# Turning h for the gate product by DMA blocks and VectorE 32x32 transposes in a gated decoder layer

## The chip, the cores and the metric

The kernel runs on one core of a Trainium2 chip. The metric is device time in microseconds of one execution; lower is better. Five engines work side by side and meet through semaphores: TensorE (PE; its weight loads are PEld), VectorE (DVE), ScalarE (ACT), GpSimd (POOL) and SyncE (SP), which here only issues DMAs. Each engine runs its own instructions in the order of the program, so one that waits holds up all that stand behind it on that engine.

## What is computed

One layer of a decoder trunk for 1024 prompt tokens and 8 sample tokens, with D = 1024, in float32. Cut to what matters here:

```python
m = sigmoid(g_a) * (y_a @ w_pa) + sigmoid(g_b) * (y_b @ w_pb)
h = h + rmsnorm(m @ w_out, post_g)
e = p @ w_ple
gate = sigmoid(rmsnorm(h, ple_in_g) @ w_pg)
h = h + rmsnorm(gate * e, ple_out_g)
```

where `rmsnorm(x, g) = x * rsqrt(mean(x * x) + 1e-6) * g` over the 1024 features. The products that make y_a, y_b, g_a and g_b come before and are not touched, save for their order on some engines.

## The kernel before

**Products.** Each float32 operand is cut into a high and a low part (`split`, L412: ACT copies, DVE subtracts), and three of the four partial products are run. Most 2x2 block products are done with seven block products instead of eight (`strassen`, L691; `strassen_within`, L740). The last two, the out product (m by w_out) and the gate product (h by w_pg), put tokens on the output partitions: the weights that PE loads are 128 x 128 blocks of m or h turned so that features lie on partitions, and w_out or w_pg stream past. Both go over four pairs of token tiles (tile t is tokens 128t to 128t+127), each pair with seven steps named by the operand they use: B11, T2, T3, T1, B21, B22, T4 (the last pair ends with B22). A step is twelve matmuls of 512 columns. `outsteps[0..3]` are followed by `gatesteps[0..3]`; `oflow` and `gflow` are these 28 and 28 steps as flat lists. The loaded weights are prepared three steps ahead (`AHEAD`): `mw` from m, `hw` from h, with `ms` and `hs` for the sums and differences. In each pair the T2 result must first have the B11 result added by DVE and be copied out by ACT before the T1 step may accumulate on it in the same PSUM region (L754 to L759).

**From the out product to the gate product.** For every token tile t the results are gathered in `h` with a sum of squares by ACT. `out_finish` (L1505) takes the root (DVE adds, POOL raises to -1/2: `rstd`, L453), scales by DVE and lets a POOL DMA add the input x in place (`accum_op`); SP then writes h to DRAM, where the last residual sum takes it from. `gate_norm` (L1514) takes the sum of squares of this h over 1024 columns by ACT, the root again, and writes `hn`, the normalised h, by ACT. `gate_input` (L1522) turns hn by eight PE transposes of 128 x 128 into two PSUM banks (`pht`), and ACT copies each bank to `big`, the buffer with features on partitions from which hw is cut. Feature k*128+p lies on partition p of row k of `big`. The rows of w_pg were multiplied by ple_in_g by ACT early on (`column_sums`, L1455, `wgraw`) and stored in DRAM as `wg`, `wglow` and `wghigh`. `gated` (L1548) applies the sigmoid to the product by ACT, multiplies by e (`eback`) by DVE, and takes the sum of squares. The 8 sample tokens (tile S) go through small matmuls of their own (`sps`), hung on steps from `oflow[OS]` and `gflow[GS]` on.

**What sets the order.** All code from the first matmul on is recorded in a `Planner` (L86). Each recorded operation has a time `at` (the PE work recorded until then), a latest time, and buffers. The planner then plays through its own durations and picks for each engine the ready operation with the least rank, `min(late, at + PATIENCE)` (L285), and may start loads `LOAD` ahead of their latest time (L274). Work hung on a step with `at(step, f)` (L1340) is recorded after that step. The order that comes out is fixed in the program; nothing is decided on the chip. 46 buffers of 128 x 1032 floats (`slot`) are handed out by the planner. Nearly every instruction has the line of the player, L354.

## Time and profile before

| what | value |
|---|---|
| time, median of three runs | 989.72 us (988.19 to 990.26) |
| the profiled execution's own time | 989.02 us |
| its span, first to last instruction | 987.3 us |
| mean granted TensorE clock | 0.998 |
| DVE, ACT, POOL busy | 793.4, 514.5, 72.6 us |
| DMA | 181.62 MB, mean 184 GB/s |

All times in what follows are those of this one profiled execution, in us from the start of its span unless a number is said to be a duration. A tile's instructions are grouped by engine and operation, with least, median and greatest duration in ns. In the chain of waits each piece is the work, or the wait, without which the last instruction would have come sooner. In the table by windows, the busy time of each engine stands beside the number of its instructions.

### The profile page before, as it was taken

What the parts mean: (1) busy time and instruction counts of PE and PEld (TensorE: products, weight loads), DVE (VectorE), ACT (ScalarE), POOL (GpSimd) and SP (SyncE); (2) the same over time, 40 slices, a digit from 0 to 9 for tenths busy, and PEclk for the clock granted to TensorE, in tenths of its full rate; (3) what the DMA queues carried; (4) which work ended last, traced back from release to release, by engine and by line L of the source; (5) the groups of instructions that cost most, each with busy time, mean ns of one, the idle gap of its engine ahead of it and who ended that gap; (6) DMA issues with size and microseconds to landing.
All of it is one profiled execution on the core that took longest, in us unless ns stands there. A gap on an engine that the chain in (4) does not pass through costs nothing.

```text
span 987.3 us, 15941 instructions
## 1 busy us (share of the span) xinstructions
PE 975.2 (99%) x6113; PEld 865.0 (88%) x6113; DVE 793.4 (80%) x1229; ACT 514.5 (52%) x861; POOL 72.6 (7%) x117
## 2 busy tenths in 40 slices
PE   8999999999999999999999999999999999999996
PEld 6889999999999999999999999999999986787765
DVE  5698469878889789887686997697799899678866
ACT  7774356766435544242332433562363364899744
POOL 1210000000000000000010100000000002222221
PEclk9999999999999999999999999999999999999999
DMA  9364654433475777441214176684582485489496
GB/s 355 135 150 87 150 127 153 150 97 122 168 275 195 277 282 253 150 162 54 87 54 153 33 240 233 242 318 158 183 302 86 167 325 133 104 268 327 104 307 193
DMA packets 123489, 181.62 MB, mean 184 GB/s; under 512 B 41222, under 2 KB 80182, under 8 KB 123405
## 3 DMA queue, kind: packets, MB, share of 16 engines
q1 hardware_dynamic: 121077, 172.71, 51.4%
q0 software_dynamic: 2048, 7.37, 4.1%
q8 instruction: 48, 0.79, 0.3%
q10 hardware_dynamic: 288, 0.52, 0.2%
q14 instruction: 28, 0.23, 0.1%
HBM read 125.08 MB, written 55.96 MB: 183 GB/s over the span
## 4 chain that ended last, share of the span: by engine, by line
PE 97%; DVE 1%; POOL 0%; ACT 0%; issue 0%; DVEq 0%; POOLq 0%
PE acc L354 73%; PE acct L354 15%; PE accm L354 2%; PE e L354 2%; PE mix L354 1%; PE sps L354 1%; PE pht L354 1%; PE pst L354 1%; POOL rstd L354 0%; DVE ge L354 0%; PE warm L354 0%; DVE hs L354 0%; DVE hw L354 0%; PE pp L354 0%; DVE wgT4l L354 0%
## 5 line engine op out<-in xcount | busy, mean ns | idle before, releaser
L354 DVE TENSOR_TENSOR u<-acc,u 128x520 f32<-128x520 f32 (+1 forms) x90 | 62.5, 695 | 33.3 <-PE acc L354 32.5
L354 POOL TENSOR_TENSOR rstd<-ms,mhalf 128x1 f32<-128x1 f32 (+1 forms) x45 | 39.6, 882 | 493.6 <-DVE ms L354 493.5
L354 ACT ACTIVATE u<-acc 128x512 f32<-128x512 f32 x39 | 23.2, 596 | 36.2 <-PE acc L354 33.7
L354 ACT ACTIVATE zbw<-zbs 128x512 fp32r<-128x512 f32 x16 | 10.0, 630 | 31.4 <-DVE zbs L354 25.6
L354 DVE TENSOR_TENSOR big<-big 128x1024 f32<-128x1024 f32 (+4 forms) x20 | 23.6, 1215 | 0.0
L354 POOL COPY big<-xb 128x1 f32<-128x1 f32 x8 | 4.0, 494 | 259.8 <-DVE zbw L354 149.4
L354 ACT ACTIVATE pbw<-pbs 128x512 fp32r<-128x512 f32 x16 | 10.1, 632 | 24.3 <-DVE pbs L354 19.0
L354 ACT ACTIVATE paw<-pas 128x512 fp32r<-128x512 f32 x16 | 10.1, 629 | 23.3 <-DVE pas L354 16.2
L354 DVE TENSOR_TENSOR zbw<-zbs,zbw 128x512 fp32r<-128x512 f32 x16 | 10.9, 688 | 13.7 <-ACT zbw L354 13.6
L354 PE MATMUL accm<-qh,wpoolw 128*128 128x260 f32 (+1 forms) x96 | 20.9, 319 | 0.0
L354 ACT ACTIVATE big<-mix 128x256 f32<-128x256 f32 x32 | 11.9, 382 | 17.0 <-PE mix L354 16.2
L354 ACT ACTIVATE gbw<-gbs 128x512 fp32r<-128x512 f32 x16 | 10.1, 630 | 16.6 <-DVE gbs L354 10.6
L354 ACT ACTIVATE u<-acct 128x512 f32<-128x512 f32 x22 | 13.0, 593 | 8.8 <-PE acct L354 5.4
L354 DVE SCALAR_TENSOR_TENSOR zb<-accm,gvec,zb 128x512 f32<-128x512 f32 (+1 forms) x16 | 12.0, 750 | 6.7 <-PE accm L354 6.4
L354 PEld LDWEIGHTS accm<-qh,wpoolw 128*128 128x128 f32 x96 | 15.6, 188 | 1.9
L354 ACT ACT_TABLE_LOAD x11 | 14.1, 1283 | 4.7 <-DMA wohigh<-woraw 1.9
L354 DVE TENSOR_TENSOR ge<-eback,ge 128x512 f32<-128x512 f32 (+2 forms) x19 | 12.4, 658 | 5.1 <-ACT ge L354 4.5
L354 ACT ACTIVATE gaw<-gas 128x512 fp32r<-128x512 f32 x16 | 10.0, 628 | 12.2 <-PE acc L354 7.5
L354 DVE TENSOR_TENSOR paw<-pas,paw 128x512 fp32r<-128x512 f32 x16 | 11.0, 687 | 6.1 <-ACT paw L354 6.1
L354 PE MATMUL mix<-wst,vh 128*128 128x256 f32 x64 | 15.5, 319 | 0.0
L354 ACT ACTIVATE gbw<-gbraw 128x512 fp32r<-128x512 f32 x12 | 7.5, 628 | 15.0 <-DMA gbraw<-in_w_in_dram 10.3
L354 ACT ACTIVATE zaw<-zas 128x512 fp32r<-128x512 f32 x16 | 10.1, 628 | 9.3 <-DVE zas L354 5.1
(664 smaller groups left out, 3575.0 us busy)
## 6 DMA issues: line engine op xcount, KB each, us to landing
ga<-ga SPq DMA_DIRECT2D x16, 516.0 KB, 7.2
gb<-gb SPq DMA_DIRECT2D x16, 516.0 KB, 7.6
ya<-za SPq DMA_DIRECT2D x8, 516.0 KB, 4.7
yb<-zb SPq DMA_DIRECT2D x8, 516.0 KB, 7.3
x<-in_x_prompt_dram SPq DMA_DIRECT2D x8, 512.0 KB, 5.6
vraw<-in_w_in_dram SPq DMA_DIRECT2D x8, 512.0 KB, 8.2
e<-e SPq DMA_DIRECT2D x8, 512.0 KB, 2.9
vturned<-v SPq DMA_DIRECT2D x32, 128.0 KB, 3.2
```

The source lines that it names most:

```text
L354: getattr(getattr(self.nc, e), method)(*(self.real(a) for a in args), **{k: self.real(a) for k, a in kwargs.items()})
```

## The change

h is no longer normalised before it is turned, and PE no longer turns it.

- `gate_input` reads h back from DRAM, where `out_finish` has put it. Four DMAs of SP per token tile, each to 32 partitions, bring 256 features each: partition 32q+f gets, for each of four groups i of 32 tokens, the 256 features from 256q on of token 32i+f. One DVE instruction then turns all 32 x 32 blocks of the tile, into `big`. So feature 256q+32k+f now lies on partition 32q+f of row k.
- The rows of w_pg are loaded in this same order, by four DMAs of 32 rows instead of one of 128 (`wgraw`), ple_in_g likewise, and for the sample tokens ACT writes hn in the new order.
- `gate_norm` takes the sum of squares in two halves of 512 columns and puts the root into a column of `hscales`; the write of hn falls away for the prompt tokens. The sigmoid takes that column as its scale, one number per token, which is a partition there.
- The steps on which the three parts are hung come from the table `TURNS`, one row per pair, as indices into `oflow + gflow`; before they were 7, 8, 13; 14, 15, 20; 21, 22, 27; 28, 29, 34. While these parts are recorded the planner's patience is 8 (`HASTE`).
- The planner's LOAD goes from 14.0 to 14.98 and PATIENCE from 60.0 to 55.8, for the whole kernel. The sample work starts two steps later in the out product and two earlier in the gate product (OS, GS), and the loads of w_pg's sums one step earlier.

```diff
+HASTE = 8.0
+TURNS = ((7, 8, 11), (14, 14, 18), (21, 26, 28), (30, 33, 35))
-OS, GS = 3, 14
+OS, GS = 5, 12
...
-    LOAD, LEAD, PATIENCE, RATE, SPARE = 14.0, 14.0, 60.0, 0.36, 3
+    LOAD, LEAD, PATIENCE, RATE, SPARE = 14.98, 14.0, 55.8, 0.36, 3
...
             op = Op(engine, len(self.ops), self.clock, self.fixed)
+            op.patience = self.patience
...
-            return min(o.late, o.at + self.PATIENCE) + (3.0 if o.table and o.table != table else 0)
+            return min(o.late, o.at + o.patience) + (3.0 if o.table and o.table != table else 0)
...
-            dma(t, src[k * P : (k + 1) * P, :])
-            if key == "wg":
+            if key == "wo":
+                dma(t, src[k * P : (k + 1) * P, :])
+            else:
+                for q in range(4):
+                    dma(t[32 * q : 32 * q + 32, :], src[(8 * q + k) * 32 : (8 * q + k + 1) * 32, :])
                 nc.scalar.activation(out=t, in_=t, func=AF.Copy, scale=col(2, k))
...
-        hn = hn_of[t] = slot("hn", (P, D))
-        rs = rstd([square_sum(h[:r], r, scratch=hn)], r)
-        nc.scalar.activation(out=hn[:r], in_=h[:r], func=AF.Copy, scale=rs[:r])
+        if t == S:
...
+            return
+        parts[t] = []
+        for j in range(2):
+            gather(parts[t], square_sum(h[:, half(j)]))
+        scales[t] = rstd(parts.pop(t), P, hscales[:, t : t + 1])
...
-        for k4 in range(0, NB, 4):
-            ps = bank("pht")
-            for k in range(4):
-                nc.tensor.transpose(ps[:, k * P : (k + 1) * P], hn[:, (k4 + k) * P : (k4 + k + 1) * P], ident)
-            nc.scalar.activation(out=big[:, k4 : k4 + 4, t * P : (t + 1) * P],
-                                 in_=ps.rearrange("p (k t) -> p k t", k=4), func=AF.Copy)
+        b, src = slot("hblocks", (P, D)), kept["h"][t * P : (t + 1) * P, :]
+        for q in range(4):
+            dma(b[32 * q : 32 * q + 32, :].rearrange("f (i c) -> f i c", i=4),
+                src[:, 2 * q * P : (2 * q + 2) * P].rearrange("(i f) c -> f i c", i=4))
+        nc.vector.transpose(out=big[:, :, t * P : (t + 1) * P].rearrange("p k (i f) -> p k i f", i=4),
+                            in_=b.rearrange("p (i k f) -> p k i f", i=4, k=NB))
...
-        nc.scalar.activation(out=g, in_=src, func=AF.Sigmoid)
+        nc.scalar.activation(out=g, in_=src, func=AF.Sigmoid, scale=1.0 if t == S else scales[t])
...
-    turn_over(wgop, [*outsteps[2][5:], *l], [*l[2:], c[0], c[1]], WITHIN)
+    turn_over(wgop, [*outsteps[2][4:], *l], [*l[2:], c[0], c[1]], WITHIN)
...
-        nxt = outsteps[i + 1] if i + 1 < NPAIR else gatesteps[0]
         ts = [2 * i + 1, 2 * i]
-        at(nxt[0], lambda ts=ts: [out_finish(t) for t in ts])
-        at(nxt[1], lambda ts=ts: [gate_norm(t) for t in ts])
-        at(nxt[6], lambda ts=ts: [gate_input(t) for t in ts])
+        for do, s in zip((out_finish, gate_norm, gate_input), TURNS[i]):
+            at((oflow + gflow)[s], lambda do=do, ts=ts: hasty(do, ts))
```

Over the whole program PE loses 64 transposes and gains nothing. DVE gains 8 transposes of 128 x 1024 and 8 instructions on one column. ACT loses 16 copies of a PSUM bank, 8 writes of hn and 8 sums of squares over 1024 columns, and gains 16 sums over 512. POOL's count stays. SP gains 32 reads of h and 24 loads of w_pg rows. The numbers behind an underscore in the rows below tell apart tiles of one name.

PE at the start of the gate product, from the B11 step of pair 0 to its T2 step, before:

```order
L354 MATMUL acct_574<-wgB11l_9299,hw_9292 128x512
L354 MATMUL acct_574<-wgB11h_9280,hw_9292 128x512
L354 MATMUL pht_570<-ident,hn_9376 128x128 x4
L354 MATMUL pht_571<-ident,hn_9376 128x128 x4
L354 MATMUL acct_579<-wgT2h_9297,hw_9344 128x512
L354 MATMUL acct_579<-wgT2l_9328,hw_9344 128x512
```

The same place of PE now:

```order
L357 MATMUL acct_569<-wgB11l_9320,hw_9285 128x512
L357 MATMUL acct_569<-wgB11h_9273,hw_9285 128x512
L357 MATMUL acct_570<-wgT2h_9294,hw_9371 128x512
L357 MATMUL acct_570<-wgT2l_9355,hw_9371 128x512
L357 MATMUL acct_570<-wgT2h_9294,hw_9371 128x512 x2
```

The eight transposes of a tile of pair 2 stood between the two steps; now the steps follow each other. The other seven groups of eight go in the same way.

DVE in the same stage, before: `acct` is the sum on the T2 result that T1 waits for, `ge_9573` the sum that frees the region of the T4 step, `h_9395` and `h_9352` the scaled h of pair 3.

```order
L354 SCALAR_TENSOR_TENSOR h_9395<-h_9395,rstd_578,post_8587 128x1024
L354 TENSOR_TENSOR hw_9426<-hs_9364,hw_9426 128x512
L354 SCALAR_TENSOR_TENSOR h_9352<-h_9352,rstd_576,post_8587 128x1024
L354 TENSOR_TENSOR wgT1l_9459<-wgT_1270_9272,wgT1h_9450 128x1024
L354 TENSOR_TENSOR wgT1l_9471<-wgT_1271_9277,wgT1h_9456 128x1024
L354 TENSOR_TENSOR acct_579<-acct_579,u_9466 128x512
L354 TENSOR_TENSOR hw_9475<-hs_9316,hw_9475 128x512
L354 TENSOR_TENSOR wgB21l_9496<-wgB_1286_9301,wgB21h_9482 128x1024
L354 TENSOR_TENSOR wgB21l_9505<-wgB_1287_9305,wgB21h_9490 128x1024
```

DVE at this place now:

```order
L357 TENSOR_TENSOR wgT1l_9418<-wgT_1260_9241,wgT1h_9341 128x1024
L357 TENSOR_TENSOR wgT1l_9429<-wgT_1261_9251,wgT1h_9377 128x1024
L357 TENSOR_TENSOR hw_9350<-hs_9337,hw_9350 128x512
L357 TENSOR_TENSOR wgB21l_9442<-wgB_1268_9277,wgB21h_9400 128x1024
L357 TENSOR_TENSOR wgB21l_9453<-wgB_1269_9283,wgB21h_9410 128x1024
L357 TENSOR_SCALAR sofar_561<-ssq_559 128x1
L357 TENSOR_SCALAR ms_562<-ssq_560,sofar_561 128x1
L357 TENSOR_TENSOR acct_570<-acct_570,u_9435 128x512
```

Pair 3's two scalings have gone from here (they stand some twenty rows further on, ahead of the first transpose of pair 2), and two cuts of B21 stand ahead of the sum on T2.

SP from the first h written to the loads of w_pg's operands, before:

```order
L354 DMA h<-h_8801 128x1024
L354 DMA h<-h_8762 128x1024
L354 DMA h<-hs_8972 8x1024
L354 DMA h<-h_8937 128x1024
L354 DMA h<-h_8990 128x1024
L354 DMA wgB_1248_9174<-wg 128x2x512
L354 DMA wgB_1249_9178<-wg 128x2x512
L354 DMA wgT_1253_9196<-wglow 128x2x512
```

SP at this place now, where `hblocks` are the reads of h, four to a tile:

```order
L357 DMA h<-h_8818 128x1024
L357 DMA h<-h_8777 128x1024
L357 DMA hblocks_8978<-h 32x4x256 x4
L357 DMA hblocks_9008<-h 32x4x256 x4
L357 DMA h<-h_8965 128x1024
L357 DMA h<-h_8953 128x1024
L357 DMA wgB_1239_9144<-wg 128x2x512
L357 DMA hblocks_9148<-h 32x4x256 x4
L357 DMA wgB_1240_9169<-wg 128x2x512
L357 DMA h<-hs_9048 8x1024
L357 DMA hblocks_9178<-h 32x4x256 x4
L357 DMA wgT_1248_9206<-wglow 128x2x512
```

Each read of a tile stands behind the write of the same tile, and loads of w_pg's operands stand behind and between the reads of pair 1.

More of the change, by code (lines that the diff above doesn't have):

```diff
@@ L44, in __init__ @@
         self.before, self.after, self.names, self.fresh = set(), [], set(), set()
-        self.late, self.ready, self.waits = None, 0.0, 0
+        self.late, self.ready, self.waits, self.patience = None, 0.0, 0, Planner.PATIENCE
 class View:
@@ L101, in __init__ @@
         self.makers, self.made, self.place = {}, {}, {}
-        self.fixed, self.open, self.clock = True, None, 0.0
+        self.fixed, self.open, self.clock, self.patience = True, None, 0.0, self.PATIENCE
         for e in self.ENGINES:
@@ L451, in gather, with rstd @@
         parts.append(part)
-    def rstd(parts, n=P):
-        t, r = sm("ms"), sm("rstd")
+    def rstd(parts, n=P, r=None):
+        t, r = sm("ms"), sm("rstd") if r is None else r
         nc.vector.tensor_scalar(out=t[:n], in0=parts[-1][:n], scalar1=EPS if len(parts) == 1 else parts[0][:n],
@@ L1141, in hybrid_step @@
     kept["e"] = dram.tile([T, D], F32, tag="e", name="e")
+    hscales, scales = cpool.tile([P, NB], F32, tag="hscales", name="hscales"), {}
     kept["wg"] = dram.tile([D, D], F32, tag="wg", name="wg")
@@ L1723, in begin @@
         for i, v in enumerate((pre_g, pool_scale, ple_in_g)):
-            dma(vecs[i * NB : (i + 1) * NB, :], v[0].rearrange("(k p) -> k p", p=P))
+            there, k = vecs[i * NB : (i + 1) * NB, :], v[0].rearrange("(k p) -> k p", p=P)
+            if i == 2:
+                there = there.rearrange("k (q f) -> k q f", q=4)
+                k = v[0].rearrange("(q k f) -> k q f", q=4, k=NB)
+            dma(there, k)
         steps[0].loads()
```

12 lines of the change are left out of this document (10 added, 2 removed).

## The prediction, made before the changed kernel was run

> **What bounds the kernel now.** I read the page's summary first, then PE's waits, then the span by windows, the late part finely.
>
> ```profile
> span 987.3 us, 15941 instructions
> PE 975.2 (99%) x6113; PEld 865.0 (88%) x6113; DVE 793.4 (80%) x1229; ACT 514.5 (52%) x861; POOL 72.6 (7%) x117
> ...
> PE warm L354 <- DVE heat L354: 1.5, 1, 1.5
> PE e L354 <- ACT wehi L354: 0.8, 1, 0.8
> PE pst L354 <- DVE x L354: 0.6, 1, 0.6
> PE acct L354 <- ACT ge L354: 0.5, 1, 0.5
> PE pht L354 <- ACT hn L354: 0.3, 1, 0.3
> PE acct L354 <- DVE ge L354: 0.3, 1, 0.3
> ...
> 20.00:300.00 280.00, 280.00 (x1866) 254.19 (x1865) 219.37 (x359) 161.57 (x276) 17.55 (x28) 1.00 0.50 149
> 300.00:400.00 100.00, 100.00 (x673) 92.17 (x671) 89.64 (x132) 49.35 (x71) 1.78 (x2) 1.00 0.70 253
> 400.00:860.00 460.00, 460.00 (x2947) 413.37 (x2947) 376.70 (x559) 199.80 (x320) 21.82 (x31) 1.00 0.49 168
> ...
> 860.00:880.00 20.00, 19.90 (x100) 16.17 (x99) 12.08 (x22) 17.72 (x33) 4.84 (x6) 1.00 0.83 264
> 880.00:900.00 20.00, 20.00 (x96) 16.22 (x95) 16.81 (x25) 17.88 (x31) 6.16 (x6) 1.00 1.05 344
> 900.00:920.00 20.00, 19.37 (x88) 15.14 (x87) 17.85 (x27) 17.87 (x29) 3.60 (x2) 1.00 0.64 178
> 920.00:940.00 20.00, 20.00 (x93) 16.33 (x92) 17.23 (x32) 15.28 (x36) 5.36 (x6) 1.00 0.61 167
> ```
>
> PE is busy for 975.2 of 987.3 us, and its waits (total, times, longest) come to 4.0 us: 2.9 while the kernel starts, 1.1 in the last 130 us. So a PE instruction that goes is time that goes, as long as nobody else becomes late by it. In the windows (length, then PE, PEld, DVE, ACT, POOL, granted clock, DMA) PE is never idle from 20 to 860 and fills almost all of each later 20 us; in those DVE has 2 to 8 us left and ACT 2 to 5. These are the engines that can take the gain back, DVE above all, since the change gives it work.
>
> **What PE loses.** The group of the turned tile, two pieces of the chain of waits, and PE's timeline around one group:
>
> ```profile
> L354 PE MATMUL pht<-ident,hn x64: 270/273/329, 847.6 to 923.6; 128*128 128x128 f32 x64
> ...
> 847.73 0.87 PE pht L354 x8
> ...
> 919.05 1.09 PE pht L354 x8
> ...
> 897.60 1.03 PE L354 MATMUL pht<-ident,hn 128*128 128x128 f32 x8
> 898.39 0.48 PE L354 MATMUL acct<-wgT3h,hw 128*128 128x512 f32 x1
> ...
> 918.34 0.39 PE L354 MATMUL acct<-wgT2h,hw 128*128 128x512 f32 x1
> 919.05 1.09 PE L354 MATMUL pht<-ident,hn 128*128 128x128 f32 x8 [0.32 <-ACT hn L354]
> ...
> 909.22 0.39 PE L354 MATMUL acct<-wgB22l,hw 128*128 128x512 f32 x1
> 909.45 0.40 PE L354 MATMUL acct<-wgB22h,hw 128*128 128x512 f32 x1
> 910.16 0.47 PE L354 MATMUL acct<-wgT4h,hw 128*128 128x512 f32 x1 [0.31 <-DVE ge L354]
> ```
>
> The 64 transposes stand in eight groups of eight, all on the chain. A group holds PE for 0.87 us there (0.79 from its first start to the next matmul, 897.60 to 898.39, and about 0.08 by which that matmul starts up more slowly): 8 x 0.87 = 7.0 us, all of it on the path. With them goes the wait at 919.05: matmuls of a step start 0.23 us apart (909.22 to 909.45) and this start came 0.71 after the one before, so 0.48 was lost. The other such place, 910.16, loses 0.71 - 0.23 = 0.48 as well, but to DVE's sum `ge`, which stays; I leave it in the sum and let the range take in that it goes.
>
> What a transpose costs is the point to settle. By its duration, 273 ns, 64 would be 17.5 us; by the distance of their starts they are 0.10 to 0.11 each, since they overlap, and it is the starts that the chain counts. The Trainium skill ("TensorE: Matmul & The Clock Gate", Part 4: PE-mode transpose) gives about 275 ns for one in a kernel; taken as a cost per transpose that would be an estimate of 17.6 us, and a time some 10 us below my forecast. The trace agrees on the duration and not on the cost; beside the chain's 0.87 for eight I give this no chance.
>
> **What the other engines get.** Rows of the same or like work:
>
> ```profile
> L354 DVE STREAM_TRANSPOSE big<-vblocks x8: 1228/1235/1248, 145.6 to 231.7; 128x1024 f32<-128x1024 f32 x8
> ...
> L354 ACT ACTIVATE hn<-h,rstd x8: 1135/1138/1151, 839.5 to 917.9; 128x1024 f32<-128x1024 f32 x8
> ...
> L354 ACT ACTIVATE big<-pht x16: 569/588/607, 848.3 to 927.6; 128x512 f32<-128x512 f32 x16
> ...
> L354 ACT ACTIVATE big<-pst,gvec x8: 679/686/690, 19.9 to 47.4; 128x512 f32<-128x512 f32 x8
> ...
> h<-in_x_prompt_dram POOLq DMA_DIRECT2D x8, 512.0 KB, 8.2
> vturned<-v SPq DMA_DIRECT2D x32, 128.0 KB, 3.2
> ...
> 897.24 2.35 DVE L354 TENSOR_TENSOR wgT1l<-wgT,wgT1h 128x1024 fp32r<-128x1024 f32 x2
> 899.51 0.69 DVE L354 TENSOR_TENSOR acct<-acct,u 128x512 f32<-128x512 f32 x1
> ...
> 900.59 0.58 ACT L354 ACTIVATE u<-acct 128x512 f32<-128x512 f32 x1
> 901.27 0.46 PE L354 MATMUL acct<-wgT1h,hw 128*128 128x512 f32 x1
> ```
>
> ACT is relieved: 16 bank copies x 0.59 = 9.4 us and 8 writes of hn x 1.14 = 9.1 go. The sums of squares in halves cost about what they did whole. The sigmoids with a scale per partition cost some 0.10 more each (686 against 588 ns for a bank with and without such a scale), 17 x 0.10 = 1.7 us. Net some 17 us less, all beside PE except the last quarter's sigmoid, which stands in the chain after the last matmul: +0.1.
>
> DVE gets 8 x 1.24 = 9.9 us of transposes, which stand in its order from the end of out pair 1 to gate pair 2, most of them in the four windows. Its room there is 7.9, 3.2, 2.2 and 2.8 us, and PE's way through them is shorter by most of the 7 us. By sums DVE still fits: from the T2 step of out pair 3 to the first of gate pair 2 I count in its order 37 instructions of 512 columns at 0.60, 14 cuts at 1.14 (half of 2.27 for two, 897.24 to 899.51), 5 scalings at 1.2, two transposes and 15 small ones, 48 us for about 55 us of PE. That is 88%, with little to spare at single places.
>
> The tightest is the sum on T2 in each pair. PE may start T1 one step after T2 ends; a step is 12 x 0.23 = 2.8 us, and DVE's sum (0.69) and ACT's copy (0.58) need 1.3 of it. Before, in gate pair 0, T2 ended at 897.60 and DVE came to it only at 899.51, 1.9 late, behind the cut of T1; the second group of transposes gave it 0.87 more, and T1 started on time at 901.27. Now this cover is gone, so DVE may be 1.5 us late and no more. For it: the two scalings of pair 3 (2 x 1.2) no longer stand ahead. Against it: the cut of B21 (2.3) and two small ones do. Adding up the rows from the cut of B11 on, I get the sum within 0.3 us of its deadline, and the first `hw` of gate pair 1, behind the two scalings and a transpose, likewise. Bounds for new waits: 0, if DVE is as early as before, and some 5 us, if each of the three nearest pairs (out pair 3, gate pairs 0 and 1) loses 1.5 us or a little more. I take 0.8, nearer to the sums of rows.
>
> **The way through DRAM.** From POOL's DMA to h turned: 8.2 (x added, median to landing), the write, four issues, the read, and the transpose. Nearest rows for the write and the reads are the 128 KB pieces of `vturned`, 3.2 us:
>
> ```profile
> 875.20 0.90 POOL L354 DMA_DIRECT2D h<-in_x_prompt_dram  x1 [0.19 <-DVE mw L354]
> 885.14 0.33 SPq L354 DMA_DIRECT2D h<-h  x1
> ```
>
> 8.2 + 3.2 + 4 x 0.33 + 3.2 + 1.2 = 17 us; with DMA as full as between 880 and 900, where the first part took 885.14 - 875.20 = 9.9, and two more such stretches, 25. The TURNS leave from out_finish to the first use, three steps before the gate step, 18 steps for pairs 0 to 2 and 16 for pair 3, 44 us or more. PE does not wait for h itself. What can wait is DVE at a transpose, and SP: its reads wait for the write, and behind them stand loads of w_pg's operands (pair 1) or of e and of the sample rows (pairs 2 and 3). For pair 1 the reads end some 10 us before PE needs T2's operand; for pair 2's second tile the read stands behind the write of pair 3's h and may come 1 to 2 us after DVE is there, with a sum behind it for which PE has a step's time. These cost nothing by rows unless the DMAs are slower by several us.
>
> The remaining edits (planner numbers, w_pg's rows in four loads, OS and GS) move work that PE does not wait for: from 20 to 860 us it shows none. I put them at 0 in the sum; the order of PE itself is the same there up to the second pair of the out product.
>
> **The sum.** 989.0 (own time of the execution: span 987.3 and 1.7 around it) - 7.0 - 0.5 + 0.1 + 0.8 = 982.4. The median of the three runs, 989.72, lies 0.7 above that execution, so I forecast 983.1. At best, with no new wait and 910.16 gone as well, 981.8; less the scatter of the runs, 981.
>
> **The rivals.**
> 1. DVE paces the gate stage: the sums on T2 and the first hw come 1 to 1.5 us late in three or four pairs. For it: DVE's 85 to 90% in the windows and no spare in my count. Against it: the waits in DVE's own order, which earlier operands shorten. It gives 3 to 5 us back: 986.
> 2. Slower: DVE stands at the transposes. If x's addition and h's write take 5 us longer each, since the reads now add 4 MB to a stretch where DMA is already full, each transpose of pairs 1 to 3 is reached before its data, and all behind it waits, the sum on T2 among it. A wait hurts PE beyond 1.5 us. Six tiles at 1.8 us each beyond that lose 10.8, and from 982.3 (the forecast without new waits) that makes 993. It decides from 7.4 lost, that is 1.2 us beyond the spare at each of six tiles. Against it: the 44 us of lead, and the place of the transposes in DVE's order.
> 3. The load of w_pg's rows is halved in speed. A tile's load lands in 3.0 to 9.3 us:
>
> ```profile
> DMA to landing us min/median/max: 3.0/3.9/9.3
> ...
> vblocks<-vturned SPq DMA_DIRECT2D x8, 512.0 KB, 3.3
> ```
>
> If pieces on 32 partitions move at half the pace, up to 9.3 us more; ACT, which scales them, would stand in front of cuts that PE needs three steps later (8.4 us at the gate's 2.8): 0.9 us at each of four pairs of loads, 3.6 in all, about 986. Against it: pieces of the same shape, `vturned`, landed in 3.2 us, a load of 512 KB to all partitions (`vblocks`) in 3.3, so four pieces in flight together need not be slower. The Trainium skill ("SBUF — State Buffer", Door 1: The DMA port swizzle) says that 32 partitions reach only 8 of 16 ports, with about half the bandwidth, and two transfers do not add up to all. By that rule this rival is the likely one; no load of that shape is in the trace of before, only the stores named, which do not show it.
> 4. No change that can be measured: reordering in the untouched stages makes waits of 5 us or more where PE now has none, and eats the gain: 989.
>
> **How the numbers follow.** Forecast (981 to 985) 0.62; rival 1 (985 to 988) 0.16; rival 3 0.04; rival 4 0.08; rival 2 0.10. About 0.2% (2 us) is what a measurement of this kernel can tell from no change. Faster by more than that: 0.62 + 0.16 + 0.04 = 0.82; within: 0.08; slower: 0.10. The range for 8 in 10 holds the forecast, rivals 1 and 3: 981 to 988.
>
> **What would show it.** Right: no PE work named pht, PE's busy time less by about 7 us, PE's waits after 860 not above 2 us, transposes of 1.24 us with h's blocks landed before DVE is there, T1 starting one step after T3. Wrong: waits of PE for DVE's acct, ACT's u or hw over 3 us in all (rival 1); DVE idle for hblocks by several us (rival 2); PE waiting between 300 and 400 us (rivals 3 and 4).

## The result and the profile after

The changed kernel takes 984.99 us by the median of eight runs (982.38 to 987.83), the kernel before 989.87 in the eight runs beside them; the ratio is 0.9956, with a 95% interval of 0.9939 to 0.9973. So it is 0.4% faster: 4.9 us by the medians and 4.4 by the ratio, where 6.6 were forecast. The profiled execution took 984.57 us, its span 982.9.

The summary on the page of the changed kernel:

```profile
span 982.9 us, 15914 instructions
PE 968.8 (99%) x6049; PEld 859.0 (87%) x6049; DVE 801.4 (82%) x1245; ACT 500.6 (51%) x853; POOL 72.0 (7%) x117
```

PE's waits there, in us: total, times, longest.

```profile
PE acct L357 <- ACT h L357: 1.9, 1, 1.9
...
PE acct L357 <- ACT ge L357: 0.6, 1, 0.6
```

And its windows (length, then PE, PEld, DVE, ACT, POOL, granted clock, DMA):

```profile
860.00:880.00 20.00, 18.10 (x76) 14.12 (x75) 11.73 (x24) 15.85 (x33) 4.27 (x7) 0.91 0.97 296
880.00:900.00 20.00, 20.00 (x88) 16.18 (x88) 19.89 (x28) 18.45 (x34) 2.23 (x3) 1.00 1.01 323
900.00:920.00 20.00, 20.00 (x87) 16.03 (x86) 19.82 (x31) 13.55 (x26) 8.87 (x5) 1.00 0.68 162
```

The group `pht` is gone, and after 860 PE waits in two places: 0.6 us in the last quarter (0.5 before), and 1.9 us at one place that the prediction did not name. The same stretch has a granted clock of 0.91. In the two windows behind it DVE is busy for 19.8 and 19.9 of 20 us, and yet PE never waits there. PE's timeline around the wait:

```profile
866.29 0.39 PE L357 MATMUL acct<-woT4h,mw 128*128 128x512 f32 x1
868.58 0.50 PE L357 MATMUL acct<-woB11h,mw 128*128 128x512 f32 x1 [1.90 <-ACT h L357]
...
872.79 0.40 PE L357 MATMUL acct<-woB11h,mw 128*128 128x512 f32 x1
873.12 0.66 PE L357 MATMUL psst<-ident,hn 8*128 8x8 f32 x8
```

The windows of 1 us that go with it:

```profile
868.00:869.00 1.00, 0.42 (x2) 0.38 (x3) 0.93 (x4) 1.00 (x3) 0.00 (x0) 1.00 0.99 245
869.00:870.00 1.00, 1.00 (x5) 0.76 (x4) 1.00 (x1) 1.00 (x3) 0.00 (x0) 0.58 1.12 199
870.00:871.00 1.00, 1.00 (x4) 0.81 (x3) 0.04 (x1) 1.00 (x4) 0.00 (x0) 0.50 0.93 246
...
872.00:873.00 1.00, 1.00 (x4) 0.55 (x3) 0.69 (x3) 0.25 (x2) 0.29 (x1) 0.71 1.06 354
```

B11 of out pair 3 starts 2.29 us after the last matmul of T4, 2.06 more than the usual 0.23. Then the step itself lasts 873.12 - 868.58 = 4.54 us instead of 2.80: for 3.5 us the granted clock reads 0.50. That is 2.06 + 1.74 = 3.8 us at one place. What PE waited for is read from the timelines of ACT, of SP and of POOL in the changed kernel:

```profile
865.51 1.06 ACT L357 ACTIVATE hn<-hs 8x1024 f32<-8x1024 f32 x1 [2.45 <-DMA hs<-in_x_sample_dram]
...
867.94 0.59 ACT L357 ACTIVATE h<-acct 128x512 f32<-128x512 f32 x1
...
865.55 0.28 SPq L357 DMA_DIRECT2D h<-hs  x1
866.00 1.73 SPq L357 DMA_DIRECT2D hblocks<-h  x4
...
858.45 0.85 POOL L357 DMA_DIRECT2D hs<-in_x_sample_dram  x1 [1.85 <-DVE hs L357]
```

The copy `h<-acct` at 867.94 frees the PSUM region that B11 needs. It stands behind the square sum over the 8 sample rows, and that one waits 2.45 us for POOL's transfer that adds x to these rows: issued at 858.45, landed 7.0 us later. Before, the same transfer left at 851.28 and took 2.8 us, with a DMA share of 0.09 meanwhile; in the changed kernel the share is 0.91 while it is under way. OS = 5 instead of 3 puts it and all the sample work off, but OS was not run by itself, and the DMAs are full at its old time as well: from 851.28 to 854.10 the share is now 0.98. SP too waits for the transfer, with its store `h<-hs`, and behind that store stand the four reads of h's blocks for the second tile of pair 1. DVE does not wait for these in this trace. It waits for h's blocks once, at the second tile of pair 2, and PE does not wait behind it:

```profile
924.51 1.25 DVE L357 STREAM_TRANSPOSE big<-hblocks 128x1024 f32<-128x1024 f32 x1 [1.54 <-DMA hblocks<-h]
```

### The profile page after: what moved, and what is told of

It reads as the page before. It is cut to its first block, busy times and chain, and to the rows that moved or that the text cites. A ratio compares the mean times of both kernels' runs of the same rounds, so it can differ in the third digit from the quotient of the medians.

```text
span 982.9 us, 15914 instructions
## 1 busy us (share of the span) xinstructions
PE 968.8 (99%) x6049; PEld 859.0 (87%) x6049; DVE 801.4 (82%) x1245; ACT 500.6 (51%) x853; POOL 72.0 (7%) x117
## 5 line engine op out<-in xcount | busy, mean ns | idle before, releaser
L357 POOL TENSOR_TENSOR rstd<-ms,mhalf 128x1 f32<-128x1 f32 (+1 forms) x37 | 29.4, 797 | 451.1 <-DVE ms L357 450.4
L357 ACT ACTIVATE big<-mix 128x256 f32<-128x256 f32 x32 | 11.9, 383 | 20.5 <-PE mix L357 19.7
L357 DVE TENSOR_TENSOR zbw<-zbs,zbw 128x512 fp32r<-128x512 f32 x16 | 10.9, 687 | 11.9 <-ACT zbw L357 11.8
L357 ACT ACTIVATE junk<-h 128x512 bf16<-128x512 f32 x25 | 15.7, 627 | 3.4 <-DVE h L357 3.0
L357 ACT ACTIVATE mw<-ms 128x512 fp32r<-128x512 f32 x16 | 10.0, 626 | 12.4 <-DVE ms L357 9.7
L357 ACT ACTIVATE xbw<-xbs 128x512 fp32r<-128x512 f32 x16 | 10.0, 626 | 11.1 <-DVE xbs L357 7.7
L357 ACT ACTIVATE uw<-us 128x512 fp32r<-128x512 f32 x16 | 10.0, 626 | 10.0 <-DVE us L357 6.0
```

The lines of the kernel that those rows point to most:

```text
L357: getattr(getattr(self.nc, e), method)(*(self.real(a) for a in args), **{k: self.real(a) for k, a in kwargs.items()})
```

## The experiments

The kernels ran in four groups, each on one chip with the kernel before beside them: 989.21 us in the first group (four kernels), 989.33 in the second (four), 988.85 in the third (three), 988.87 in the fourth (one). Each time is a median over 5 to 12 executions, and each kernel has one profile. Across groups the ratios to before are what is compared; the changed kernel's is 0.9956.

### The norm of the sample rows later (first group)

```diff
-    at(oflow[OS + 12], lambda: gate_norm(S))
-    at(oflow[OS + 15], lambda: gate_input(S))
+    at(oflow[OS + 18], lambda: gate_norm(S))
+    at(oflow[OS + 21], lambda: gate_input(S))
```

> The changed kernel with the sample tile's norm and gate input handed to the planner six out steps later. Theory A (a square sum on ACT that stands in front of a bank copy waits for POOL's adding transfer of the 8 sample rows): the square sum now stands behind the copy of acct that B11 of out pair 3 waits for, so PE's wait of 1.9 us at that step goes, and the 1.7 us by which that step runs slower after the wait go with it: 3.8 us better than the changed kernel, about 981 by the median, and a PE wait at that place of at most 0.3 us. Rival B (the bank copy is late because ACT and DVE have too much to do there, whoever stands in front): the wait stays at 1 to 2 us, 984 to 985. Rival C (the slow matmuls of that step come from the granted clock of 0.91 in this stretch and not from the wait): the wait goes, but the step still lasts about 4.5 us instead of 2.8, about 983.

Measured: 989.24 us (986.43 to 993.65), ratio 1.0004 (0.9992 to 1.0016). The wait at B11 is gone and the step lasts 2.77 us, as theory A and not B or C has it; the time is 8 us above what A had. In the profile (its fastest run) PE waits for ACT's `u` at T1 of gate pairs 0, 1 and 2, 2.2 us in all. PE's T1 of gate pair 0 and DVE ahead of it, in this kernel's timeline:

```profile
896.40 0.50 PE L357 MATMUL acct<-wgT1h,hw 128*128 128x512 f32 x1 [0.79 <-ACT u L357]
...
891.83 2.35 DVE L357 TENSOR_TENSOR wgB21l<-wgB,wgB21h 128x1024 fp32r<-128x1024 f32 x2
...
894.70 0.70 DVE L357 TENSOR_TENSOR acct<-acct,u 128x512 f32<-128x512 f32 x1
```

T2 ended at 892.66 and DVE came to its sum 2.0 us later, behind the cut of B21: the place that the prediction had feared. These waits are not all: from PE's last matmul to the end of the span it takes 11.4 us instead of 8.7. This run moved more than it meant to. The planner put all that follows into another order, so it can't tell whether the loss comes from PE being early or from the new order.

### The sample rows' x added by DVE (first group)

```diff
-        nc.gpsimd.dma_start(out=h, in_=x_of(t), accum_op=ALU.add)
+        if t == S:
+            xs = slot("xs", (P, D))
+            dma(xs[:r], x_of(t))
+            add(h, h, xs[:r])
+        else:
+            nc.gpsimd.dma_start(out=h, in_=x_of(t), accum_op=ALU.add)
```

> The changed kernel with the 8 sample rows of x loaded ahead by SP and added by DVE, instead of by POOL's adding transfer. Nothing is put off. Theory A (what ACT waits for is that transfer, 7.0 us from issue to landing here): ACT's square sum over the sample rows waits for DVE alone, and PE's wait of 1.9 us at B11 of out pair 3 goes with the slow step behind it: about 981. The added work is one addition of 8 by 1024 on DVE, some 1.2 us by the nearest rows, in a stretch where DVE has 8 of 20 us left. Rival B (ACT is late at that copy for other reasons): the wait stays, 984 to 985.5.

Measured: 992.29 us (987.84 to 997.34), ratio 1.0028 (1.0010 to 1.0047). Again no wait at B11, and again the gain is not there: the new order has B21 ahead of T1 in pair 3, and PE stands 3.67 us for T1's result. T1's last matmul started at 883.01; ACT came to the copy only at 886.45, behind `wgT1h`, before which it had stood 1.31 us for DVE's `hs`. PE's row and, 16 us earlier, DVE's first transpose of pair 1, in this kernel's timeline:

```profile
887.08 0.50 PE L357 MATMUL acct<-woB22h,mw 128*128 128x512 f32 x1 [3.67 <-ACT u L357]
...
871.46 1.25 DVE L357 STREAM_TRANSPOSE big<-hblocks 128x1024 f32<-128x1024 f32 x1 [2.37 <-DMA hblocks<-h]
```

The window two us later reads a clock of 0.50 again:

```profile
889.00:890.00 1.00, 1.00 (x4) 0.78 (x3) 1.00 (x3) 1.00 (x3) 0.00 (x0) 0.50 1.05 404
```

And DVE now stands 2.37 us for h's blocks, the kind of wait that rival 2 of the prediction has; that PE's wait comes of it is not shown.

### Each PE transpose twice, in the kernel before (first group)

```diff
-            for k in range(4):
-                nc.tensor.transpose(...)
+            for _ in range(2):
+                for k in range(4):
+                    nc.tensor.transpose(...)
```

> The kernel before with each of the 64 PE transposes of h done twice into the same place, so that the price of a transpose is measured by itself. By the distance of their starts, as the prediction takes it (0.79 to 0.87 us for a group of eight): 64 more cost 6.3 to 7.0 us, 996 to 997 by the median, and PE's busy time grows by as much. By their duration (273 ns each, nothing overlapped): 17.5 us more, about 1007. If ACT's copies behind them are late as well, up to 0.5 us more for each group, 1000.

Measured: 995.89 us (995.65 to 995.94), ratio 1.0065 (1.0053 to 1.0077): 6.7 us for 64, 0.10 us each. The group in this kernel:

```profile
L354 PE MATMUL pht<-ident,hn 128*128 128x128 f32 x128 | 15.3, 273 | 0.2 <-ACT hn L354 0.2
```

One piece of its chain of waits:

```profile
847.93 1.75 PE pht L354 x16
```

Sixteen hold PE for 1.75 us where eight held it 0.87. A transpose still lasts 273 ns; by that it would have been 17.5 us.

### The rows of w_pg loaded whole (first group)

```diff
-                for q in range(4):
-                    dma(t[32 * q : 32 * q + 32, :], src[(8 * q + k) * 32 : (8 * q + k + 1) * 32, :])
+                dma(t, src[k * P : (k + 1) * P, :])
```

> The changed kernel with each tile of w_pg's rows loaded by one transfer to 128 partitions, as before the change, instead of four to 32 partitions each. The rows then stand in the old order while h and ple_in_g stand in the new one, so the gate product is another sum of the same size. Theory A (the four pieces cost nothing that PE sees, since ACT's longer wait for them, 7.3 us four times against 3.7 three times before, lies beside PE's work): the same time as the changed kernel, 984 to 986, and landing times of 3 to 9 us. Rival 3 of the prediction (pieces on 32 partitions move at half the pace and PE pays): 1 to 4 us faster than the changed kernel, 981 to 984, with ACT's waits for w_pg's rows back at 4 us in all.

Measured: 984.65 us (983.12 to 987.25), ratio 0.9954 (0.9941 to 0.9968), the changed kernel's own. ACT's waits for these rows, first of the changed kernel, then of this one, and the landing times:

```profile
  DMA wgraw<-in_w_pg_dram: 7.3, 4
...
DMA to landing us min/median/max: 2.6/6.2/8.0
```

```profile
  DMA wgraw<-in_w_pg_dram: 4.1, 2
...
DMA to landing us min/median/max: 2.6/6.5/9.9
```

ACT waits 3.2 us more with the four pieces and PE not at all; a piece of 128 KB on 32 partitions lands no sooner than the whole tile of 512 KB, but no later either. Neither profile has a PE wait for these rows or for what is cut from them, so rival 3 is out.

### Four more matmuls in front of the wait (second group)

Into the planner's player, just ahead of the last matmul of T4 in out pair 2:

```diff
+                if args and self.extra is not None and args is self.extra[1]:
+                    for _ in range(4):
+                        o, w, x = (self.real(a) for a in args)
+                        self.nc.tensor.matmul(o[:NS], self.zeros.bitcast(F32R), x, start=False, stop=False, ...)
```

> The changed kernel with four more matmuls of 512 columns on TensorE (an 8-column operand of zeros, added to what is there, so nothing changes in the result) just ahead of the last one of T4 in out pair 2, which is the work before PE's wait at B11 of out pair 3. Everything else keeps its place. The end of that wait is set by ACT and a DMA and not by PE, so PE stands idle 0.9 us less, about 1.0 instead of 1.9. Theory A (what makes the B11 step last 4.5 us instead of 2.8 is that PE stood idle for 1.9 us; the waits of 0.3 to 1.4 us in the other two runs were followed by steps of ordinary length): the step is 2.8 to 3.0 us long, PE's clock stays at 1.0 in the rows there, and the later steps start 1.7 us sooner, so that four more matmuls make the kernel faster, about 983.3, unless VectorE's sums on T2 then come late and take it back as in the runs with the wait removed. Rival B (the step is slow because of what else runs there, DMA and the other engines): it lasts 4.5 us again and the time is that of the changed kernel, 985.

Measured: 983.48 us (982.17 to 984.77), ratio 0.9938 (0.9926 to 0.9949). B11 starts 0.24 us after T4, lasts 2.85 us, and the clock reads 1.00 all through. Four matmuls more cost nothing, as A has it. That a wait of 1.9 us makes the step slow is not tested by this profile: here the 8 rows landed in 5.7 us and ACT stood 1.14 us for them, much as in the next run, where PE's wait was 0.7 us and the step of ordinary length without any added matmul. That they gain is not shown by the median either: the unedited kernel in the same group (next) had 983.51. The spread is less, 2.6 us over 5 executions against 6.2 over 7. In this profile PE also waits 1.2 us for DVE's `za` at 382.58, in a stage that the change does not touch.

### The changed kernel once more (second group)

> The changed kernel once more, for a second profile of it. Theory A (PE's wait at B11 of out pair 3 comes from the order of ACT's queue and the landing of the sample rows, so it is there in every execution and its length varies with the DMA): the wait is again there, 0.5 to 3 us, the median 984 to 986. Rival B (the wait was a chance of that one execution): no wait at B11, and the same median, so that the gain is limited by other places.

Measured: 983.51 us (982.20 to 988.35), ratio 0.9950 (0.9932 to 0.9968). The profiled execution took 982.30. Its row at B11 in the timeline:

```profile
867.86 0.50 PE L357 MATMUL acct<-woB11h,mw 128*128 128x512 f32 x1 [0.71 <-ACT h L357]
```

The wait is there again, for the same `h` of ACT, and ACT waits again for the sample rows, 1.26 us instead of 2.45; the step lasts 2.98 us. The gate stage is as on time as in the first profile. So theory A holds, though the median lies 0.5 us below its range. The two executions differ by 984.57 - 982.30 = 2.3 us; at this one place it is 3.8 against 0.9 + 0.2, and 0.5 us go the other way before the out product.

### The old placing, with the new way of h (second group)

```diff
-HASTE = 8.0
-TURNS = ((7, 8, 11), (14, 14, 18), (21, 26, 28), (30, 33, 35))
-OS, GS = 5, 12
+HASTE = 55.8
+TURNS = ((7, 8, 13), (14, 15, 20), (21, 22, 27), (28, 29, 34))
+OS, GS = 3, 14
...
-    turn_over(wgop, [*outsteps[2][4:], *l], [*l[2:], c[0], c[1]], WITHIN)
+    turn_over(wgop, [*outsteps[2][5:], *l], [*l[2:], c[0], c[1]], WITHIN)
```

> The changed kernel with all of its placing put back: TURNS (7,8,13), (14,15,20), (21,22,27), (28,29,34), OS and GS 3 and 14, no haste for the h work, w_pg's operand loads one step later. The way of h through DRAM, the VectorE transposes and the planner's numbers stay. Theory A (the transposes taken from PE are the gain, and the placing decides how much of it ACT and DVE take back): the gain is still there in part, but other places wait, 984 to 990. Rival B (putting off the h work of late pairs is what pays): 989 or more, with DVE idle for hblocks by several us, since for pair 3 the reads then have three steps less. Rival C (the placing doesn't matter): 985, within 1.

Measured: 994.87 us (989.25 to 996.77), ratio 1.0046 (1.0029 to 1.0062): slower than before the change. PE's longest wait, with DVE's and ACT's ahead of it, in this kernel's timeline:

```profile
890.86 0.79 PE L357 MATMUL acct<-wgB11h,hw 128*128 128x512 f32 x1 [3.83 <-DVE sofar L357]
...
885.44 1.23 DVE L357 TENSOR_TENSOR wgT3l<-wgT,wgT3h 128x1024 fp32r<-128x1024 f32 x1 [2.88 <-ACT wgT3h L357]
...
884.35 1.06 ACT L357 ACTIVATE wgT3h<-wgT 128x1024 fp32r<-128x1024 f32 x1 [4.12 <-issue]
```

So the placing is worth some 9 us here, with the planner's numbers that were chosen for the new one. Between the two profiles it is 8.0: 3.8 are this wait, 1.6 the slower step behind it, 4.3 lie behind PE's last matmul (13.0 us to the end instead of 8.7) and some 2 at other places, while the 3.8 us at B11 of out pair 3 fall away. ACT's stand of 4.1 us ahead of wgT3h has no releaser in the profile. But a load of these operands lands just then, at 872.38 + 11.9 = 884.28, so this load is the likely cause:

```profile
L357 SPq DMA_DIRECT2D wgT<-wghigh x1: 377/377/377, 872.4 to 872.4; - x1
...
DMA to landing us min/median/max: 11.9/11.9/11.9
```

The edit issues these loads one step later. DVE nowhere waits for h's blocks in this profile, so rival B's time came by another way than B's. At B11 of out pair 3 PE does not wait: the transfer for the sample rows leaves at 850.54 and lands in 3.4 us. Since all of the placing went back together, that does not single out OS.

### The planner's two numbers alone, in the kernel before (second group)

```diff
-    LOAD, LEAD, PATIENCE, RATE, SPARE = 14.0, 14.0, 60.0, 0.36, 3
+    LOAD, LEAD, PATIENCE, RATE, SPARE = 14.98, 14.0, 55.8, 0.36, 3
```

> The kernel before with the planner's two numbers alone changed (LOAD 14.0 to 14.98, PATIENCE 60.0 to 55.8). The prediction put them at nothing: 989 to 990. Rival 4 of the prediction (reordering costs PE waits where it now has none): 991 or more. If they bring a part of the gain: 988 or less.

Measured: 991.41 us (989.45 to 993.12), ratio 1.0018 (1.0009 to 1.0027), 1 to 3 us slower, the time that rival 4 has here. The stretch that rival 4 named, 300 to 400 us, has a PE wait of 0.3 where it had none; the largest is in the out product, in PE's timeline at B22 of pair 3, for ACT's copy of T1:

```profile
887.74 0.50 PE L354 MATMUL acct<-woB22h,mw 128*128 128x512 f32 x1 [1.19 <-ACT u L354]
```

### The planner's two numbers put back, in the changed kernel (third group)

The same line of the diff the other way round.

> The changed kernel with the planner's two numbers put back (LOAD 14.0, PATIENCE 60.0), the counterpart of the run in which they alone were changed and cost 2.1 us. Theory A (neither set is better in itself; each was fitted to an order, and a change of them orders the late stage anew, with waits at other places): 985 to 992, with PE waits after 860 of over 2 us at places where the changed kernel has none. Rival B (the numbers cost 2 us here as well, in the stages that the change does not touch): 982 to 983.5. Rival C (they don't matter): 983.5 to 985.

Measured: 993.33 us (991.00 to 995.71), ratio 1.0041 (1.0028 to 1.0054). That is above the range of theory A, and in no other's. PE waits four times for `za` and `u` between 342 and 386, 3.2 us in all, and in the late part for `u` (five times, 3.0 us) and once for `hw` (1.7). The late waits are those that A has. But against the changed kernel's profile 5.2 us are lost before the out product starts, in stages that the change does not touch, 1.6 from there to PE's last matmul, and 4.2 behind it. So it is borne out that neither set is better in itself, but most of the loss lies outside the out and gate products, where A put it. The wait for `hw` is of use for the clock. PE's row before it and its own, in this kernel's timeline:

```profile
917.68 0.39 PE L357 MATMUL acct<-wgT2l,hw 128*128 128x512 f32 x1
919.74 0.72 PE L357 MATMUL acct<-wgT2h,hw 128*128 128x512 f32 x2 [1.67 <-DVE hw L357]
```

The window behind it:

```profile
920.00:921.00 1.00, 1.00 (x6) 0.79 (x6) 1.00 (x3) 0.37 (x2) 0.37 (x1) 1.00 0.74 82
```

PE stood for 1.67 us here and went on at full clock; the windows from 921 to 923 read 1.00 as well.

Four runs so far had the planner order things anew. Their profiles against the changed kernel's, in us more or less:

| run | before the out product | out and gate product, to PE's last matmul | behind it |
|---|---|---|---|
| norm of the sample rows later | 0.0 | -0.8 | +2.7 |
| x added by DVE | +1.7 | +4.3 | +2.1 |
| old placing | 0.0 | +3.7 | +4.3 |
| old numbers | +5.2 | +1.6 | +4.2 |

Each loses 2 to 4 us after PE has done its last matmul; what makes that stretch longer was not followed up.

### The norm put behind, and nothing else moved (third group)

Rows moved in the planner's finished order; on ACT, and on PE and DVE alike (the eight small transposes `psst` behind T2, their copy `sst` behind the sum on T2):

```diff
-ACTIVATE hn,ssq<-hs 8x1024
 ACTIVATE junk,ssq<-h 128x512
 ACTIVATE junk,ssq<-acct 128x512
 ACTIVATE h<-acct 128x512
-ACTIVATE hn<-hs,rstd 8x4x8x32
+ACTIVATE hn,ssq<-hs 8x1024
 ACTIVATE junk,ssq<-acct 128x512
 ACTIVATE h<-acct 128x512
+ACTIVATE hn<-hs,rstd 8x4x8x32
```

> The changed kernel with the sample rows' norm alone put behind in the engines' queues, by hand, and not one other instruction moved: on ACT the square sum over the sample rows stands behind the copy of acct that B11 of out pair 3 waits for, and its scaling behind the next copy; on PE the eight small transposes stand behind T2 instead of B11; on VectorE their copy behind the sum on T2. Theory A (that queue place on ACT makes PE's wait of 0.7 to 1.9 us and, where the wait is long, the slow step behind it; the run that put the norm off by the planner lost the gain because all that follows was ordered anew): the wait goes, no step lasts 4.5 us, the later steps keep the order in which they were on time, and the time is 980.5 to 982, with the runs close together, within 3 us. Rival B (PE arriving 1 to 4 us earlier finds VectorE's sums on T2 late, whatever their order): waits of PE for ACT's u at T1 of gate pairs 0 to 2, 1 us or more in all, and 983.5 to 989.

Measured: 984.24 us (981.68 to 986.24), ratio 0.9952 (0.9938 to 0.9966), a time in rival B's range. B11 starts on time and no step lasts 4.5 us. But three steps later PE stands 1.52 us at T1, and at 888.28 (B11 of gate pair 0) it is where the second profile of the unedited kernel is, at 888.21. PE's row, DVE's for the second tile of pair 1 and for the sum, and SP's, in this kernel's timeline:

```profile
877.04 0.50 PE L388 MATMUL acct<-woT1h,mw 128*128 128x512 f32 x1 [1.52 <-ACT u L388]
...
873.34 1.25 DVE L388 STREAM_TRANSPOSE big<-hblocks 128x1024 f32<-128x1024 f32 x1 [2.30 <-DMA hblocks<-h]
...
875.67 0.69 DVE L388 TENSOR_TENSOR acct<-acct,u 128x512 f32<-128x512 f32 x1
...
864.44 0.40 SPq L388 DMA_DIRECT2D h<-hs  x1
865.01 2.29 SPq L388 DMA_DIRECT2D hblocks<-h  x4
```

Neither theory as it was written: what DVE waits for in front of the sum on T2 is h's blocks (B's waits in the gate stage are there too, but only 0.5 us at one T1). SP's store of the sample rows, at 864.44, had waited for the same 8 rows, and the reads stand behind it. A third theory followed: one transfer of 32 KB holds two queues. But the second profile of the unedited kernel has the store at the same place, and there the reads went out no sooner, 1.48 us after the start of T4 of out pair 2 against 1.55 here, and DVE did not wait. What differs is how long these four reads took to land, first there, then here:

```profile
DMA to landing us min/median/max: 3.9/4.1/4.3
```

```profile
DMA to landing us min/median/max: 6.2/6.3/6.3
```

The reads of the first tile, issued before any moved row had its turn, were slower here as well, 5.8 us at the median against 4.5. So most of this wait comes of slower landing in this one execution, and why it was slower stays open.

### Each DVE transpose twice (third group)

```diff
+            flow = [(e, call) for e, call in self.order()
+                    for _ in range(2 if call[0] == "transpose" and e == "vector"
+                                   and call[2]["in_"].tensor.name[:7] == "hblocks" else 1)]
```

> The changed kernel with each of the eight VectorE transposes of h done twice in a row into the same place, nothing else moved: 8 x 1.24 = 9.9 us more work on VectorE. Theory A (VectorE has room for the transposes, up to the spare that the prediction worked out for the sums on T2, 0.3 us here and a few elsewhere): some waits of PE of 0.5 to 1.2 us at T1 or at hw in the pairs where a transpose stands ahead, 2 to 5 us in all: 986 to 989. Rival 1 of the prediction (VectorE paces the gate stage): all of the added work shows, 993 to 995. If VectorE had ample room: 985 or less.

Measured: 990.86 us (988.71 to 992.69), ratio 1.0020 (1.0011 to 1.0028): 6 us for 9.9 us of work, a little above theory A's range and below rival 1's. Most of it is one place in its timeline, T1 of out pair 3:

```profile
883.12 0.68 PE L360 MATMUL acct<-woT1h,mw 128*128 128x512 f32 x1 [4.36 <-ACT u L360]
...
872.75 2.52 DVE L360 STREAM_TRANSPOSE big<-hblocks 128x1024 f32<-128x1024 f32 x2 [2.95 <-DMA hblocks<-h]
```

Here too the wait for h's blocks comes first, and the doubled work behind it. With the slow step behind the wait T1 of out pair 3 loses 6.2 us, T1 of out pair 2 loses 1.4, gate pairs 1 and 2 lose about 1.2 and 0.6, gate pair 0 nothing. That is 9.4 us, nearly as much as the added work; it comes to 6 net because PE, arriving later, waits only 0.3 us at B11 of out pair 3, so that 3.2 of the 3.8 us there are not lost. So DVE's room is less than the net time suggests.

### The norm put behind, and the store too (fourth group)

The kernel with the norm put behind, and on SP:

```diff
 DMA hblocks<-h 32x4x256 x4
 DMA wgB<-wg 128x2x512
-DMA h<-hs 8x1024
 DMA hblocks<-h 32x4x256 x4
+DMA h<-hs 8x1024
```

> The kernel of the run before with the norm put behind, and one more instruction moved: on SP the store of the sample rows' h, which waits for the same adding transfer of 8 rows, stands behind the four reads of h's blocks for the second tile of pair 1 instead of ahead of them. In that run PE no longer waited at B11, but VectorE stood 1.0 and 2.3 us for h's blocks, the sum on T2 of out pair 3 came late by it, and PE stood 1.5 us at T1 instead. Theory A (the landing of the 8 rows holds two queues, ACT's and SP's; only with both freed does the gain stay): the reads go out about 1.8 us sooner, VectorE's wait for the second tile falls from 2.3 to about 0.5 us, PE's wait at T1 of out pair 3 to 0.5 us or less, and the time is 1 us below that run's, 981 to 983.3. Rival B (DMA is full there and the blocks land as late as before): VectorE's wait stays at 2 us and the time at 984. Rival C (the sums on T2 in the gate stage, where VectorE is full, take it back): T1 of out pair 3 is on time, but PE waits 1 us or more at T1 of gate pairs 0 and 1, 983.5 to 985.

Measured: 982.32 us (981.24 to 983.82), ratio 0.9934 (0.9921 to 0.9948), the lowest ratio of the study. DVE's transpose of the second tile, its sum on T2, and SP's rows, in this kernel's timeline:

```profile
872.27 1.25 DVE L392 STREAM_TRANSPOSE big<-hblocks 128x1024 f32<-128x1024 f32 x1 [1.27 <-DMA hblocks<-h]
...
874.60 0.69 DVE L392 TENSOR_TENSOR acct<-acct,u 128x512 f32<-128x512 f32 x1
...
865.47 1.77 SPq L392 DMA_DIRECT2D hblocks<-h  x4
867.34 0.28 SPq L392 DMA_DIRECT2D h<-hs  x1
```

DVE's wait fell from 2.30 to 1.27 us, less than A had, but enough: T1 of out pair 3 starts on time, and after it PE waits 0.3 us at one T1 and 0.6 in the last quarter. Time and waits are as theory A has them; its mechanism is shown only in part. Counted from the start of T4 of out pair 2, the blocks were there 2.1 us sooner than in the run before, and the last of the four reads had gone out 1.1 us sooner; the rest is that they landed in 4.9 us instead of 6.2 to 6.3. The interval overlaps that of the changed kernel (0.9939 to 0.9973) and that of the run with the norm alone (0.9938 to 0.9966), so its lead, 2 us by the ratios over either, is likely and not certain; the spread is 2.6 us over 5 executions against 5.5 over 8.

## Why the prediction was right, and which term was not

- **The transposes, -7.0.** Right. Doubling them cost 6.7 us, and by the rows 0.10 us each and not 0.27. What the page of the Trainium skill gives for one ("TensorE: Matmul & The Clock Gate", Part 4: PE-mode transpose, about 275 ns) is its duration here too, and not its price in a row of eight.
- **The wait at 919.05, -0.5.** Right, gone. The other one, at 910.16, which the sum left in, went as well: 0.5 better than the sum.
- **The last sigmoid, +0.1.** Nearly right: PE's wait there grew from 0.47 to 0.56, and the stretch from PE's last matmul to the last instruction's end by 0.1 more. No term was there for the last store, whose landing took 0.4 us longer; the out product had started 0.4 earlier, and the two cancel.
- **New waits, +0.8.** This is the term that was mis-sized, and in the wrong place. The sums on T2 in the gate stage, where it was put, were on time in both profiles of the changed kernel. The wait that came was 2.06 + 1.74 = 3.8 us at B11 of out pair 3. With it goes the step that failed: "OS and GS ... move work that PE does not wait for", at 0. The new placing has a transfer of 8 rows land in 7.0 us instead of 2.8, and ACT's square sum behind it holds a copy that PE needs; the run with that norm alone put behind, where B11 starts on time, shows it. That OS by itself does it is not shown. The prediction counted what stands behind h's reads on SP, but not what stands behind the sample rows on ACT.
- **The other numbers at 0.** The loads in four pieces: right, 984.65 without them. LOAD and PATIENCE: not 0 by themselves. Alone they cost 2 us, and without them the changed kernel loses 8.
- **The balance** of the profiled execution: 982.4 + 3.8 - 0.8 - 0.5 = 984.9 against 984.57. The median lies 0.4 above that execution, where the forecast took 0.7.
- **The signs.** PE's busy time fell by 6.4 us (7.9 in the second profile), where about 7 was said. PE's waits after 860 came to 2.5 us (1.3), where 2 was the most. Seven of eight transposes found h's blocks landed. The eighth, pair 2's second tile, stood 1.54 us (1.81): the prediction gave it 1 to 2, at no cost, and PE did not wait.
- **Rival 2, DVE at the transposes.** Its mechanism is there, at that tile, and at pair 1 in the run with the norm alone put behind: 2.3 us, with blocks that took 6.2 to 6.3 us to land. It never reached the size that decides.
- **Rival 4, waits in the untouched stages.** Not in the two profiles of the changed kernel: up to 860 us PE waits no more than before by over 0.6 us. But in three profiles of kernels with the same order up to there PE waits for DVE's `za` at about 382 us: 1.2 us with four more matmuls, 1.0 with each DVE transpose twice, 0.5 with the store put behind too.
- **Rival 1, DVE paces.** Not in the changed kernel; near it. With 9.9 us more work on DVE the new losses come to 9.4 us, 6 net. The two runs that gave the sample rows' work other orders lose 5 and 7 us against the changed kernel, but in their profiles 2 to 3 of these lie behind PE's last matmul.

Why the runs of the changed kernel spread over 5.5 us is shown for two of them alone: with the landing of 8 rows in 5.8 or 7.0 us, 1.1 or 3.8 us are lost at B11. For the others there is no trace; the wait at 382 us may have a part in it.

## What to carry to other kernels

Before putting off a piece of work, follow each of its instructions into the queue where it then stands, the small ones too: here 8 rows of 1024 held ACT, and behind it a PSUM copy. A wait that goes may only uncover the next one, so look at what the engines behind it wait for then; and before naming its cause, see in a second profile whether the same order has that wait at all. And where an order comes from a planner, test a cause by moving the instructions themselves; a change of the planner's inputs moves everything behind it, and two such runs here came out 5 and 7 us slower with the suspected wait gone.

## What was not expected of the hardware

- **A PE wait has a second price.** Behind idle times of 1.90, 3.67, 3.83 and 4.36 us the granted clock read 0.50 for some 3.5 us, and the twelve matmuls of the next step took 4.38 to 4.54 us instead of 2.8: 1.6 to 1.7 us on top. Behind 1.52 and 1.67 us it read 1.00 and the matmuls kept their usual pace. The Trainium skill ("TensorE: Matmul & The Clock Gate", HAM oscillation) sets the limit at idle gaps of about 3.4 us. The half clock agrees; if the idle time alone decides, the limit in these six cases lies between 1.67 and 1.90.
- **A small adding transfer can take as long to land as a large one.** It took 2.8 us with a DMA share of 0.09 and 7.0 with a share of 0.91. A full DMA does not always cost it that much: with shares of 0.81 to 0.98 in other profiles it took 3.4 to 6.4 us. The 32 KB of the sample rows, before and after, and the median of POOL's 512 KB ones after:

```profile
hs<-in_x_sample_dram POOLq DMA_DIRECT2D x1, 32.0 KB, 2.8
```

```profile
hs<-in_x_sample_dram POOLq DMA_DIRECT2D x1, 32.0 KB, 7.0
...
h<-in_x_prompt_dram POOLq DMA_DIRECT2D x8, 512.0 KB, 6.1
```
